# One hybrid decoder trunk, one core: recurrent output scaled in one run, query copies on their own condition, and an order planned with VectorE held while GpSimd works

## The chip, the core and the metric

The program runs on one core of one Trainium2 chip. The figure is the device time of one execution, in microseconds; for the kernel before it is 2374.19 us, the median of three runs from 2373.58 to 2376.77. In the profile the engines are PE (TensorE matmuls), PEld (its weight loads), DVE (VectorE), ACT (ScalarE), POOL (GpSimd) and SP (SyncE, here only a queue that issues transfers).

## The reference

T = 1040 tokens (16 learned ones in front of 1024) of 1024 features pass two layers, in float32.

```python
for l in range(DEPTH):
    hn = rms_norm(h, norm_mix_g[l]); proj = hn @ w_in[l]
    q, k, v, xr, gate = jnp.split(proj, splits, axis=-1)   # 512 columns each
    q = apply_partial_rope(rms_norm(q, q_norm_g[l]), cos, sin)      # 4 heads x 2 x 64; k alike
    o_attn = diff_attention(q, k, v, lam)      # softmax(q1 k1) - lam * softmax(q2 k2), causal, times v
    o_rec = rms_norm(rg_lru_branch(xr, gate, ...), rec_norm_g[l])
    h = h + jnp.concatenate([rms_norm(o_attn, ...) * (1 - lam_init), o_rec], axis=-1) @ w_out[l]
    hn = rms_norm(h, norm_ffn_g[l]); g, u = jnp.split(hn @ w_gu[l], [D_FF], axis=-1)
    h = h + (silu(g) * u) @ w_down[l]
return h[:, N_META:, :]
```

The recurrent branch is a four-tap convolution, two gates (`r`, `ig`), the scan h[t] = a[t] h[t-1] + u[t] over the tokens, a product with gelu(gate), and the norm over its 512 features with gain `rec_norm_g`.

## The kernel before, in words

**Products.** Features lie on the partitions, tokens along the free axis, in three chunks of 348, 348 and 344 columns; attention works in nine blocks of 116 tokens. Each float32 matmul is three passes over a high and a low part (`hn0h`, `hn0l` of the activations, `wh`, `wl` of the weights): high by high, low by high, high by low. One tile of a projection (`pxr`, `pgt`, `pq`, `pk`, `pv` of 128 columns and one chunk) is 24 matmuls of some 0.16 us each. High parts are made by ACT, low parts by DVE or POOL.

**Stages of a layer.** The input projections of the recurrent branch; its gates, scan and gelu; then, on the same PE queue, q, k and v of head 0; then four heads, each with its scores, softmax and value products, between which q, k, v of the next head are projected; the output projection; the FFN as seven half-size products in place of eight. In layer 0 the attention begins at about 150 us and ends at about 530, in layer 1 at about 1310 and 1740.

**Norms.** Squares are summed by tiny matmuls with a column of ones (`st_r` for the first norm, `st_q`, `st_k`, `st_y` for queries, keys and the recurrent output), the root is taken on DVE in a chain of tiny operations, and a matmul with the identity spreads it over the partitions (`bc_r`, `bck`, `bc_y`). `row` is the spread root as a tile of 128 x 1040: first that of the layer's norm, then that of the recurrent output. For a head, ACT takes the squares `csqq`, `csqk` and a scaled copy `crawq`, `crawk` out of PSUM; DVE shuffles them (`cshq`, `cshk`), POOL does the two products of the rotation with `sin` and `cos`, DVE adds them; ACT makes the high part `qh`, DVE the low part `ql`. The squares of the recurrent output are taken by ACT into one place, `sq_accy`, and summed by DVE into `accy`; so each `sq_accy` waits until DVE has added the one before.

**What sets the order.** Every piece of work is a generator, run by a `Planner` when the program is built. It keeps an assumed clock for each engine (`busy`, line 181), events, places for tiles (`get`, `free`, `lend`, `give`) and a patience for kinds of work (`turn`, with the table TURN; `idle` waits until the assumed clock of an engine stands still). Its assumed costs decide nothing but the order in which instructions are written. Each engine then executes its own instructions strictly in that order; a stalled instruction holds all behind it.

**The recurrent output** (`rec_norm`, from line 1431). hs0 to hs3 are the four blocks of 128 features. For each block in the order YN = [1, 2, 3, 0] and each chunk, DVE multiplies the block by `row` (from the second block on only when the planner's DVE clock stands still), ACT and DVE split it into a high and a low part `yo`, and POOL issues a transfer `yd<-yo` to DRAM. A block's tile then becomes a place for something else: hs2 and hs3 a second `vh` and `vl`, hs0 a second set of probability tiles `P1`, hs1 two more places for query copies (`both`). When the last chunk is out, the `row` tile becomes one more place for the tile P08, the probabilities of the last block. YO is the order in which the output projection reads the blocks.

**The query copies** (`twice`, from line 1159, in `attention`). For each block of 116 queries six transfers on the SP queue write both 64-row halves of the queries into a `view` or `both` tile that the scores `S` read. `twice` is started inside `attention`, behind a wait for the head's finished keys, queries and roots.

Of the kernel before, what the change touches and what calls it, by code (L numbers as in the profile page):

```python
# [18 lines left out]
T = 1040  # L19
# [75 lines left out]
YN = [1, 2, 3, 0]  # L95
YO = [1, 2, 0, 3]
# [37 lines left out]
class Planner:  # L134
# [5 lines left out]
    def __init__(self):  # L140
        self.heap, self.seq, self.now = [], 0, 0.0
        self.clock = {}
        self.held, self.live = {}, 0
# [37 lines left out]
    def busy(self, eng, cost, after=0.0):  # L181
        start = max(self.now, self.clock.get(eng, 0.0), after)
        self.clock[eng] = start + cost
        return start + cost

# [67 lines left out]
def nblk(i):  # L253
    return min(BQ, T - i * BQ)
# [3 lines left out]
def trunk_kernel(ctx: ExitStack, tc: tile.TileContext, h0, win, wout, wgu, wdn,  # L258
# [56 lines left out]
    def tt(out_, in0, in1, op, after=0.0, eng="V"):  # L315
        (V if eng == "V" else G).tensor_tensor(out=out_, in0=in0, in1=in1, op=op)  # L316
        n = cols(out_)
        return ready(eng, n * 1.042 + 68 if eng == "V" else n * 2.1 + 148, after)
# [8 lines left out]
    def stt(out_, in0, s, in1, op0, op1, after=0.0):  # L327
        V.scalar_tensor_tensor(out=out_, in0=in0, scalar=s, in1=in1, op0=op0, op1=op1)  # L328
        return ready("V", cols(out_) * 1.042 + 70 + 60 * aps(s), after)
# [488 lines left out]
    class Layer:  # L818
        def __init__(self, l):
# [6 lines left out]
            self.ev_q = [Event() for _ in range(HEADS)]  # L826
            self.ev_k = [Event() for _ in range(HEADS)]
# [97 lines left out]
    def qk_task(L, h, which, evs):  # L925
# [8 lines left out]
        if which == "q":  # L934
            yield from S.wait(*evs["st"])
# [3 lines left out]
            yield from S.wait(*evs["ch"])  # L939
# [151 lines left out]
    def attention(L, h):  # L1091
        yield from S.wait(L.ev_att, L.ev_q[h], L.ev_k[h], L.ev_vecs)
        l, cb, vt = L.l, L.cb, L.vt
        q, k, cq = L.q[h].parts, L.k[h].parts, L.cq[h]
        views, ev_b, nleft = {}, [Event() for _ in range(NB)], {}
# [63 lines left out]
        def twice():  # L1159

            yield from S.wait(L.ev_both[h])
            for b in range(NB):
                v = yield from S.take(L.both)
                mq = nblk(b)
                qs = slice(b * BQ, b * BQ + mq)
                for cc in range(2):
                    rows = slice(64 * cc, 64 * cc + 64)
                    for i, r in ((0, 0), (0, 64), (1, 64 * cc)):  # L1170
                        e = dma(nc.sync, v[r:r + 64, i, cc, :mq].bitcast(F32), q[i][rows, qs].bitcast(F32), 256 * mq)
                nleft[b] = 2
                views[b] = v
                S.set(ev_b[b], e)
            S.set(L.ev_both[h + 1])

# [10 lines left out]
        S.start(twice())  # L1187
# [146 lines left out]
    def rec_blocks(L):  # L1334
# [8 lines left out]
        def block(b):  # L1343
# [55 lines left out]
            e = S.busy("V", T * 2.13 + 10)  # L1399
# [36 lines left out]
    def rec_norm(L):  # L1436
# [9 lines left out]
        yield from S.wait(L.ev_att)  # L1446
        for b in YN:
            for c, (c0, cw) in enumerate(CH):
                y = L.hs[b][:, c0:c0 + cw]
                if b != YN[0]:  # L1450
                    yield from S.idle("V")
                e = tt(y, y, L.row[:, c0:c0 + cw], ALU.mult)
# [895 lines left out]
```

## Time and profile before

| | us |
|---|---|
| median of 3 runs | 2374.19 (2373.58 to 2376.77) |
| the profiled execution, its own time | 2380.8 |
| its span, first to last instruction | 2378.6 |
| PE busy | 2291.9 (96%) |
| DVE busy | 1864.1 (78%) |
| ACT / POOL busy | 1074.4 / 416.9 |
| mean granted TensorE clock | 0.979 |

The profiled execution took 6.6 us longer than the median of the timed runs, and 2.2 us of its time lie outside the span. Since PE is busy for nearly all of it, the useful readings are the stretches in which PE is not busy or in which it got a lower clock, and what PE waited for there.

### The profile page before, as it was taken

To read this page: it belongs to the slowest core of one execution; us is meant where nothing else is said; L and a number is where in the kernel's file an instruction comes from. 1 tells how busy PE (TensorE), PEld (TensorE's weight loads), DVE (VectorE), ACT (ScalarE), POOL (GpSimd) and SP (SyncE) were. 2 spreads that over 40 slices of the span, in tenths; PEclk is the share of its full clock that TensorE was granted. 3 is DMA by queue.
4 is the path that set the end of the run, shared out by engine and by line. 5 is a ranking of instruction groups with operands and counts; after the bars stand their busy time and mean duration, and the time that the engine had idled before them with its cause. 6 is when DMAs were issued, how large, how long until landed. Compare 5 with 4: busy or idle time off the path is not lost.

```text
span 2378.6 us, 40752 instructions
## 1 busy us (share of the span) xinstructions
PE 2291.9 (96%) x14514; PEld 2125.6 (89%) x14514; DVE 1864.1 (78%) x4392; ACT 1074.4 (45%) x2090; POOL 416.9 (18%) x611
## 2 busy tenths in 40 slices
PE   7998999998999999999999999999899999999998
PEld 7998898998999999999999889988688888888887
DVE  7888898888888877755976878987888888776565
ACT  4655564554333332444547555654533333335442
POOL 4134322100121200000000443230001211000000
PEclk8999999999999999999999899999999999999999
DMA  3114336323565422756521143273335654238554
GB/s 124 60 36 127 87 85 211 116 101 115 197 208 191 167 98 99 263 189 202 197 83 57 48 125 96 72 225 102 112 133 204 213 178 150 98 129 292 177 185 157
DMA packets 186539, 339.36 MB, mean 143 GB/s; under 512 B 54120, under 2 KB 75290, under 8 KB 186336
## 3 DMA queue, kind: packets, MB, share of 16 engines
q1 hardware_dynamic: 153760, 227.57, 30.1%
q0 software_dynamic: 32576, 109.19, 12.8%
q8 instruction: 114, 1.87, 0.3%
q14 instruction: 89, 0.73, 0.1%
HBM read 219.72 MB, written 95.64 MB: 133 GB/s over the span
## 4 chain that ended last, share of the span: by engine, by line
PE 80%; DVE 14%; ACT 2%; issue 2%; DMA 1%; SPq 1%; DVEq 0%; POOL 0%; ACTq 0%; POOLq 0%
PE pd L297 29%; PE pb L297 16%; PE pa L297 13%; PE po L297 3%; PE pgt L297 3%; PE pxr L297 3%; PE pv L297 3%; PE S L297 2%; PE pq L297 2%; PE pvo L297 2%; DVE P L1120 1%; PE pk L297 1%; PE atr L301 1%; PE pga L297 1%; DVE P L328 1%
## 5 line engine op out<-in xcount | busy, mean ns | idle before, releaser
L297 PE MATMUL pd<-rf,wh 128*128 128x260 f32 (+1 forms) x1848 | 414.4, 319 | 0.0
L297 PEld LDWEIGHTS pd<-rf,wh 128*128 128x128 f32 x1848 | 305.7, 188 | 27.5
L297 PE MATMUL pd<-rf,wl 128*128 128x260 f32 (+1 forms) x924 | 295.9, 320 | 0.0
L297 PEld LDWEIGHTS pd<-rf,wl 128*128 128x128 f32 x924 | 173.8, 188 | 13.8
L332 POOL DMA_DIRECT2D ad<-ct x154 | 83.0, 540 | 578.4 <-DVE ct L316 571.7
L307 ACT ACTIVATE P<-P,mx,cq 116x232 f32<-116x232 f32 (+6 forms) x144 | 124.9, 870 | 77.4 <-DVE mx L328 69.6
L316 DVE TENSOR_TENSOR ct<-pd,ct 128x260 f32<-128x260 f32 (+1 forms) x204 | 102.5, 512 | 70.8 <-PE pd L297 68.9
L297 PE MATMUL pa<-B11h,fA 128*128 128x260 f32 (+1 forms) x528 | 128.3, 324 | 19.2 <-ACT B11h L307 19.2
L316 DVE TENSOR_TENSOR ct<-pb,ct 128x260 f32<-128x260 f32 (+1 forms) x198 | 101.4, 512 | 53.9 <-PE pb L297 52.2
L316 POOL TENSOR_TENSOR wl<-wr,wh 128x512 fp32r<-128x512 f32 x70 | 97.3, 1405 | 193.2 <-ACT wh L307 163.2
L297 PE MATMUL pb<-B22h,fS 128*128 128x260 f32 (+1 forms) x528 | 126.6, 321 | 0.0
L297 PE MATMUL pb<-T1h,fS 128*128 128x260 f32 (+1 forms) x528 | 126.2, 321 | 0.0
L297 PE MATMUL pa<-B21h,fA 128*128 128x260 f32 (+1 forms) x528 | 125.7, 320 | 0.4 <-ACT ct L307 0.4
L297 PE MATMUL pb<-T2h,fS 128*128 128x260 f32 (+1 forms) x528 | 126.0, 320 | 0.0
L297 PE MATMUL pd<-T3h,fS 128*128 128x260 f32 (+1 forms) x528 | 125.9, 319 | 0.0
L297 PE MATMUL pd<-T4h,fA 128*128 128x260 f32 (+1 forms) x528 | 125.3, 319 | 0.0
L316 DVE TENSOR_TENSOR ct<-ct,ct 128x520 f32<-128x520 f32 (+2 forms) x171 | 115.9, 682 | 6.9 <-DMA ad<-ct 3.3
L297 PEld LDWEIGHTS pa<-B11h,fA 128*128 128x128 f32 x528 | 90.3, 191 | 27.5 <-ACT B11h L307 19.9
L297 PEld LDWEIGHTS pa<-B21h,fA 128*128 128x128 f32 x528 | 88.9, 188 | 8.4 <-ACT ct L307 0.9
L297 PEld LDWEIGHTS pb<-T2h,fS 128*128 128x128 f32 x528 | 89.4, 189 | 7.7
L297 PEld LDWEIGHTS pb<-T1h,fS 128*128 128x128 f32 x528 | 89.0, 188 | 7.9
L307 ACT ACTIVATE ah<-atr 116x348 fp32r<-116x348 f32 (+1 forms) x144 | 57.2, 409 | 86.0 <-PE pvo L297 46.0
(392 smaller groups left out, 7121.4 us busy)
## 6 DMA issues: line engine op xcount, KB each, us to landing
wr<-in_win_dram SPq DMA_DIRECT2D x80, 256.0 KB, 2.8
ad<-ct POOLq DMA_DIRECT2D x77, 260.0 KB, 2.7
ad<-ct POOLq DMA_DIRECT2D x77, 256.0 KB, 2.8
ct<-in_wgu_dram SPq DMA_DIRECT2D x64, 256.0 KB, 3.2
ht<-in_wgu_dram SPq DMA_DIRECT2D x60, 256.0 KB, 3.9
sq<-ad SPq DMA_DIRECT2D x58, 260.0 KB, 4.8
sq<-ad SPq DMA_DIRECT2D x58, 256.0 KB, 5.2
hw<-in_wgu_dram SPq DMA_DIRECT2D x48, 256.0 KB, 2.7
```

The costliest lines, as they stand in the source:

```text
L297: PE.matmul(out_, lhsT=lhsT, rhs=rhs, start=start, stop=stop, **(dict(skip_group_check=True) if on else {}))
L301: PE.transpose(out_, in_, idn)
L307: A.activation(out=out_, in_=in_, func=func, **kw)
L316: (V if eng == "V" else G).tensor_tensor(out=out_, in0=in0, in1=in1, op=op)
L328: V.scalar_tensor_tensor(out=out_, in0=in0, scalar=s, in1=in1, op0=op0, op1=op1)
L332: eng.dma_start(out=out_, in_=in_)
L1120: V.tensor_tensor_reduce(out=pt[:mq, k0:k0 + kw], in0=sc[:mq, :kw], in1=mask, scale=1.0, scalar=NEG if i == 0 else mx[:mq, cc, i - 1:i], o ...
```

## The change

Five things are edited.

- `YN` and `YO` become [1, 0, 2, 3]: the blocks of the recurrent output are finished, and read by the output projection, in that order.
- In `rec_norm` all twelve products with `row` come first, before the wait for the pools of the attention (`ev_att`); each takes its turn by TURN instead of waiting for a still DVE. Right behind them the tile `row` is lent to P08. The splits and transfers follow in a second loop. The first two blocks, not only the first, are staged in the places of P05 to P07.
- In the planner, POOL's tensor_tensor operations leave their assumed start and end in `S.shared`, and `behind` makes a DVE tensor_tensor or scalar_tensor_tensor whose two inputs both lie in SBUF, and the scan, start only after such an operation that is then running. This is in the plan alone: no instruction and no wait on the chip is added by it, only the order changes, for the whole program.
- `twice` is started at the head of `attention` and waits for the pools, for the previous head's copies and for a new event `ev_qt`, set when the query tiles are written. It no longer waits for the keys, the recurrent branch's vectors or the query roots.
- `row` is no longer lent at the end of `rec_norm`.

```diff
@@ -92,8 +92,8 @@
 RB = [RA, RQ, RA, RQ]
 
 YS = {2: ("vh", 1), 3: ("vl", 1), 0: ("P1", NP1), 1: None}
-YN = [1, 2, 3, 0]
-YO = [1, 2, 0, 3]
+YN = [1, 0, 2, 3]
+YO = [1, 0, 2, 3]
 NXR, NGT = 1, 5
 HR = [("r", "xr", 1), ("r", "xc", 2), ("r", "xc", 2), ("r", "r", 1), ("r", "ig", 1), ("r", "a", 1), ("r", "e2", 1),
       ("y", "hs2", 1), ("y", "hs3", 1)]
@@ -140,6 +140,7 @@
     def __init__(self):
         self.heap, self.seq, self.now = [], 0, 0.0
         self.clock = {}
+        self.shared = []
         self.held, self.live = {}, 0
 
     def start(self, gen, at=None):
@@ -183,6 +184,12 @@
         self.clock[eng] = start + cost
         return start + cost
 
+    def behind(self, after=0.0):
+
+        start = max(self.now, self.clock.get("V", 0.0), after)
+        self.shared = [x for x in self.shared if x[1] > self.now]
+        return max([start] + [b for a, b in self.shared if a <= start < b])
+
     def slots(self, pool, tag, bufs):
         if tag not in pool.slots:
             pool.slots[tag] = Slots([(0.0, pool, tag, bufs)] * bufs)
@@ -315,7 +322,13 @@
     def tt(out_, in0, in1, op, after=0.0, eng="V"):
         (V if eng == "V" else G).tensor_tensor(out=out_, in0=in0, in1=in1, op=op)
         n = cols(out_)
-        return ready(eng, n * 1.042 + 68 if eng == "V" else n * 2.1 + 148, after)
+        if eng == "V":
+            if not (in_psum(in0) or in_psum(in1)):
+                after = S.behind(after)
+            return ready(eng, n * 1.042 + 68, after)
+        e = ready(eng, n * 2.1 + 148, after)
+        S.shared.append((S.clock["G"] - n * 2.1 - 148, S.clock["G"]))
+        return e
 
     def ts(out_, in0, s1, s2, op0, op1=None, after=0.0, eng="V"):
         kw = {} if op1 is None else dict(op1=op1)
@@ -326,6 +339,8 @@
 
     def stt(out_, in0, s, in1, op0, op1, after=0.0):
         V.scalar_tensor_tensor(out=out_, in0=in0, scalar=s, in1=in1, op0=op0, op1=op1)
+        if not (in_psum(in0) or in_psum(in1)):
+            after = S.behind(after)
         return ready("V", cols(out_) * 1.042 + 70 + 60 * aps(s), after)
 
     def dma(eng, out_, in_, nbytes):
@@ -824,6 +839,7 @@
             self.q = [Block() for _ in range(HEADS)]
             self.k = [Block() for _ in range(HEADS)]
             self.ev_q = [Event() for _ in range(HEADS)]
+            self.ev_qt = [Event() for _ in range(HEADS)]
             self.ev_k = [Event() for _ in range(HEADS)]
             self.ev_v = [Event() for _ in range(HEADS)]
             self.ev_pv = [Event() for _ in range(HEADS)]
@@ -932,11 +948,12 @@
         S.start(qk_open(L, h, which, evs["tiles"]))
         S.set(evs["open"])
         if which == "q":
+            yield from S.wait(*evs["ch"])
+            S.set(L.ev_qt[h])
             yield from S.wait(*evs["st"])
             L.cq[h] = yield from S.get(small, "cq", 3, [BQ, NB, 2], F32, f"cq{l}_{h}")
             yield from rsqrt(L.cq[h], U.ss, [BQ, NB, 2], f"q{l}_{h}")
             S.free(S.now, U.ss)
-            yield from S.wait(*evs["ch"])
             S.set(L.ev_q[h])
             return
         for c in range(3):
@@ -1089,10 +1106,31 @@
 
 
     def attention(L, h):
+        views, ev_b, nleft = {}, [Event() for _ in range(NB)], {}
+
+        def twice():
+
+
+
+            yield from S.wait(L.ev_att, L.ev_qt[h], L.ev_both[h])
+            q = L.q[h].parts
+            for b in range(NB):
+                v = yield from S.take(L.both)
+                mq = nblk(b)
+                qs = slice(b * BQ, b * BQ + mq)
+                for cc in range(2):
+                    rows = slice(64 * cc, 64 * cc + 64)
+                    for i, r in ((0, 0), (0, 64), (1, 64 * cc)):
+                        e = dma(nc.sync, v[r:r + 64, i, cc, :mq].bitcast(F32), q[i][rows, qs].bitcast(F32), 256 * mq)
+                nleft[b] = 2
+                views[b] = v
+                S.set(ev_b[b], e)
+            S.set(L.ev_both[h + 1])
+
+        S.start(twice())
         yield from S.wait(L.ev_att, L.ev_q[h], L.ev_k[h], L.ev_vecs)
         l, cb, vt = L.l, L.cb, L.vt
         q, k, cq = L.q[h].parts, L.k[h].parts, L.cq[h]
-        views, ev_b, nleft = {}, [Event() for _ in range(NB)], {}
         lsum = yield from S.get(small, "lsum", 2, [BQ, NB, 2], F32, f"lsum{l}_{h}")
         G.memset(lsum, 1.0)
         a_ev = [Event() for _ in range(NB)]
@@ -1156,24 +1194,6 @@
 
         left = [NB]
 
...
         def all_scores():
             yield from S.wait(L.ev_p1[h])
             for qb in range(NB):
@@ -1184,7 +1204,6 @@
                 S.start(block(qb, tiles[qb], P1, None))
             S.set(L.ev_p1[h + 1])
 
-        S.start(twice())
         S.start(all_scores())
         yield from S.wait(L.ev_v[h])
         v = L.v[h]
@@ -1396,7 +1415,7 @@
             hs = yield from S.get(L.cy, f"hs{b}", 1, [P, WY[b]], F32, f"hs{l}_{b}")
             hs = hs[:, :T]
             V.tensor_tensor_scan(out=hs, data0=a, data1=ig, initial=0.0, op0=ALU.mult, op1=ALU.add)
-            e = S.busy("V", T * 2.13 + 10)
+            e = S.busy("V", T * 2.13 + 10, S.behind())
             S.free(e, a, ig)
             L.hs[b] = hs
             S.set(L.ev_hs[b], e + LAT)
@@ -1443,15 +1462,23 @@
         S.set(L.ev_rec2)
         yield from S.wait(*there)
         S.free(S.now, ry)
-        yield from S.wait(L.ev_att)
+
+        scaled = {}
         for b in YN:
             for c, (c0, cw) in enumerate(CH):
                 y = L.hs[b][:, c0:c0 + cw]
-                if b != YN[0]:
-                    yield from S.idle("V")
-                e = tt(y, y, L.row[:, c0:c0 + cw], ALU.mult)
-                yield e + LAT
-                tag = f"P0{5 + c}" if b == YN[0] else "oh"
+                yield from S.turn("V", "r")
+                scaled[b, c] = tt(y, y, L.row[:, c0:c0 + cw], ALU.mult) + LAT
+        yield from S.wait(L.ev_att)
+        S.lend(S.clock["V"], const, "row", S.slots(L.cb, f"P0{NB - 1}", 0))
+        for b in YN:
+            for c, (c0, cw) in enumerate(CH):
+                y = L.hs[b][:, c0:c0 + cw]
+                if b not in YN[:2]:
+                    yield from S.turn("V", "r")
+                if scaled[b, c] > S.now:
+                    yield scaled[b, c]
+                tag = f"P0{5 + c}" if b in YN[:2] else "oh"
                 st = yield from S.get(L.cb, tag, 1, [P, 2, CW], F32R, f"yo{l}_{b}{c}")
                 e = yield from split(st[:, 0, :cw], st[:, 1, :cw], y, L.vt[:, V_REC + b:V_REC + b + 1], kind="r")
                 yield e + LAT
@@ -1464,7 +1491,6 @@
                 for i in range(2):
                     place_view(L, both[:, i])
             S.set(L.ev_y[b], e)
-        S.lend(e, const, "row", S.slots(L.cb, f"P0{NB - 1}", 0))
 
 
     def open_layer(L):
```

No instruction is added or removed as work (PE has 11738 rows in both programs), but the order moves everywhere. Three places show how. A row is line, operation, written tile, read tiles, shape.

**The start, DVE.** `hn0l` is the low part of the normed input; its number names the eighth of the features (109, 111, ... 123) and the tile it reads names the chunk (`hr_133`, `hr_135` chunk 0, `hr_144`, `hr_146`, `hr_148` chunk 1, `hr_150`, `hr_153`, `hr_156` chunk 2). In the program before, the low parts of chunk 1 stand together:

```order
L328 SCALAR_TENSOR_TENSOR hn0l_109<-hr_144,vec_87,hn0h_108 128x348
L328 SCALAR_TENSOR_TENSOR hn0l_111<-hr_144,vec_87,hn0h_110 128x348
L328 SCALAR_TENSOR_TENSOR hn0l_113<-hr_144,vec_87,hn0h_112 128x348
L328 SCALAR_TENSOR_TENSOR hn0l_115<-hr_146,vec_87,hn0h_114 128x348
L328 SCALAR_TENSOR_TENSOR hn0l_117<-hr_146,vec_87,hn0h_116 128x348
L328 SCALAR_TENSOR_TENSOR hn0l_121<-hr_148,vec_87,hn0h_120 128x348
L328 SCALAR_TENSOR_TENSOR hn0l_119<-hr_146,vec_87,hn0h_118 128x348
L328 SCALAR_TENSOR_TENSOR hn0l_123<-hr_148,vec_87,hn0h_122 128x348
```

In the changed program the eighth numbered 119 of chunk 1 (`hn0l_119<-hr_146`) stands 18 rows further back, behind a stretch that holds chunk 2's parts, the root of chunk 0 (`ms_r`, `re`, `rr`, `nq_r`) and the low part `gwl` of a gate weight. The last of it reads:

```order
L335 TENSOR_SCALAR rr_106<-ms_r_302 116x3
L341 SCALAR_TENSOR_TENSOR hn0l_123<-hr_148,vec_87,hn0h_122 128x348
L323 TENSOR_TENSOR nq_r_315<-rr_106 116x3
L341 SCALAR_TENSOR_TENSOR hn0l_121<-hr_156,vec_87,hn0h_120 128x344
L323 TENSOR_TENSOR nq_r_315<-nq_r_315,ms_r_302 116x3
L341 SCALAR_TENSOR_TENSOR hn0l_111<-hr_150,vec_87,hn0h_110 128x344
L341 SCALAR_TENSOR_TENSOR nq_r_315<-nq_r_315 116x3
L323 TENSOR_TENSOR gwl_190<-wr_0_307,gwh_189 128x512
L341 SCALAR_TENSOR_TENSOR rr_106<-nq_r_315,rr_106 116x3
L323 TENSOR_TENSOR gwl_190<-wr_1_311,gwh_189 128x512
L341 SCALAR_TENSOR_TENSOR nq_r_315<-rr_106 116x3
L341 SCALAR_TENSOR_TENSOR hn0l_119<-hr_146,vec_87,hn0h_118 128x348
```

PE's matmuls of `pxr_01` (chunk 1) with `hn0h_118` and `hn0l_119`, which stood at its rows 64 to 66, stand at 73 to 75, behind the nine sums `st_r` of chunk 0.

**The opening of layer 0's attention, ACT.** Before, the squares `csqk` of the first two chunks of keys stand behind squares of the recurrent output (`sq_accy`) and high parts of the queries (`qh`), which wait for DVE:

```order
L307 ACTIVATE sq_accy_1517<-hs_2_1428 128x348
L307 ACTIVATE qh_0_1360<-crawq_01_1446 128x348
L307 ACTIVATE sq_accy_1545<-hs_2_1428 128x344
L307 ACTIVATE sq_accy_1561<-hs_3_1391 128x348
L307 ACTIVATE csqk_00_1563<-pk_00_1486 128x348
L307 ACTIVATE crawk_00_1564<-pk_00_1486,vec_87 128x348
L307 ACTIVATE qh_0_1360<-crawq_00_1404 128x348
L307 ACTIVATE sq_accy_1581<-hs_3_1391 128x348
L307 ACTIVATE qh_0_1360<-crawq_02_1501 128x344
L307 ACTIVATE sq_accy_1615<-hs_3_1391 128x344
L307 ACTIVATE csqk_01_1627<-pk_01_1553 128x348
L307 ACTIVATE crawk_01_1628<-pk_01_1553,vec_87 128x348
```

After:

```order
L314 ACTIVATE csqq_02_1498<-pq_02_1437 128x344
L314 ACTIVATE crawq_02_1500<-pq_02_1437,vec_87 128x344
L314 ACTIVATE sq_accy_1505<-hs_2_1423 128x348
L314 ACTIVATE csqk_00_1545<-pk_00_1485 128x348
L314 ACTIVATE crawk_00_1546<-pk_00_1485,vec_87 128x348
L314 ACTIVATE qh_0_1360<-crawq_00_1404 128x348
L314 ACTIVATE sq_accy_1565<-hs_2_1423 128x348
L314 ACTIVATE qh_0_1360<-crawq_01_1448 128x348
L314 ACTIVATE csqk_01_1602<-pk_01_1535 128x348
L314 ACTIVATE crawk_01_1603<-pk_01_1535,vec_87 128x348
L314 ACTIVATE sq_accy_1606<-hs_2_1423 128x344
```

The squares of key chunk 0 now stand behind one `sq_accy` and no `qh`, those of chunk 1 behind one more `sq_accy` and two `qh`; the rest of `sq_accy` is behind them. PE's order follows: `st_y`, the sums over `accy`, moves from its rows 809 to 817 to rows 885 to 892, behind the value projection. In layer 1 ACT's order changes in the same way.

**The scores of head 0 in layer 1, PE.** `S_0010` and `S_0000` are the scores of block 0. Before, they stand in the second query tile of head 1 (`pq_11`):

```order
L297 MATMUL pq_11_16557<-hnh_2_13146,wl_16285 128x348
L297 MATMUL pq_11_16557<-hnh_3_13148,wh_16284 128x348
L297 MATMUL pq_11_16557<-hnl_3_13149,wh_16284 128x348
L297 MATMUL pq_11_16557<-hnh_3_13148,wl_16285 128x348
L297 MATMUL S_0010_16583<-kl_0_16037,view_16256 116x116 x2
L297 MATMUL S_0000_16586<-kh_0_16036,view_16256 116x116 x2
L297 MATMUL pq_11_16557<-hnh_4_13937,wh_16284 128x348
L297 MATMUL pq_11_16557<-hnl_4_13938,wh_16284 128x348
```

After, they stand 62 rows later, between the first and the second key tile of head 1:

```order
L304 MATMUL pk_10_16607<-hnh_7_14433,wh_16415 128x348
L304 MATMUL pk_10_16607<-hnl_7_14434,wh_16415 128x348
L304 MATMUL pk_10_16607<-hnh_7_14433,wl_16416 128x348
L304 MATMUL S_0010_16684<-kl_0_16031,view_16386 116x116 x2
L304 MATMUL S_0000_16687<-kh_0_16030,view_16386 116x116 x2
L304 MATMUL pk_11_16692<-hnh_0_13142,wh_16415 128x348
L304 MATMUL pk_11_16692<-hnl_0_13143,wh_16415 128x348
L304 MATMUL pk_11_16692<-hnh_0_13142,wl_16416 128x348
```

In layer 0 they stand at row 950 in both. The scores of block 8 of head 0, whose probabilities use the place lent from `row`, move from PE's row 1335 to 1191 in layer 0, and from 8326 to 8217 in layer 1.

More of the change, by code (lines that the diff above doesn't have):

```diff
@@ L1157, in attention @@
         left = [NB]
[L1159 to L1175, printed above, removed]
         def all_scores():
```

## The prediction

> **What bounds the kernel now.** First the page's head, busy times and the chain that ended last:
>
> ```profile
> span 2378.6 us, 40752 instructions
> PE 2291.9 (96%) x14514; PEld 2125.6 (89%) x14514; DVE 1864.1 (78%) x4392; ACT 1074.4 (45%) x2090; POOL 416.9 (18%) x611
> PE 80%; DVE 14%; ACT 2%; issue 2%; DMA 1%; SPq 1%; DVEq 0%; POOL 0%; ACTq 0%; POOLq 0%
> ```
>
> PE is idle for 2378.6 - 2291.9 = 86.7 us, and all work on it stays. So a gain can only come from that idle time, or from time at a low clock. Next the windows (start and end, length, busy us of PE, PEld, DVE, ACT, POOL, then granted clock, DMA share, GB/s):
>
> ```profile
> 0.00:60.00 60.00, 47.19 (x228) 44.19 (x229) 44.87 (x98) 25.07 (x46) 26.81 (x30) 0.86 0.38 124
> 60.00:150.00 90.00, 89.68 (x569) 89.01 (x568) 70.13 (x96) 63.17 (x93) 17.23 (x16) 1.00 0.16 51
> 150.00:190.00 40.00, 34.04 (x207) 32.54 (x205) 36.47 (x109) 17.58 (x41) 21.95 (x29) 0.87 0.25 71
> 190.00:560.00 370.00, 343.69 (x2331) 335.53 (x2330) 315.83 (x1061) 203.97 (x456) 90.27 (x120) 0.96 0.39 119
> 560.00:1300.00 740.00, 740.00 (x6008) 739.92 (x6006) 565.70 (x1119) 300.11 (x546) 73.86 (x141) 1.00 0.48 162
> 1320.00:1360.00 40.00, 35.18 (x193) 34.50 (x191) 35.01 (x97) 14.61 (x33) 19.82 (x22) 0.79 0.13 36
> 1360.00:1680.00 320.00, 301.50 (x1932) 280.87 (x1932) 260.81 (x949) 173.60 (x411) 89.87 (x120) 0.98 0.40 119
> ```
>
> From 60 to 150 and from 560 to 1300 PE works without a gap: these stretches pass a shift on, unchanged. The losses lie in four places: the start; layer 0's opening of attention (150 to 190: 40 - 34.04 = 5.96 us idle, and 13% of 34 busy us, 4.4, to the clock); layer 1's (1320 to 1360: 4.82 idle, 21% of 35.2, 7.4, clock); and the heads between. The change's order moves work in all four.
>
> **The start.** The timeline of 17 to 57 us (start, length, engine, line, operation; in brackets the idle time ahead and what ended it):
>
> ```profile
> 17.31 16.53 DVE L328 SCALAR_TENSOR_TENSOR hn0l<-hr,vec,hn0h 128x348 fp32r<-128x348 f32 x14
> 25.04 10.74 POOL L316 TENSOR_TENSOR hr<-hr 128x1044 f32<-128x1044 f32 x8 [0.95 <-DVE hn0l L328]
> 37.12 0.56 DVE L328 SCALAR_TENSOR_TENSOR hn0l<-hr,vec,hn0h 128x344 fp32r<-128x344 f32 x1
> 36.51 0.68 DVE L316 TENSOR_TENSOR wl<-wr,wh 128x512 fp32r<-128x512 f32 x1
> 33.75 0.32 PE L297 MATMUL pxr<-hn0h,wl 128*128 128x344 f32 x1
> 39.37 3.25 PE L297 MATMUL st_r<-sums,hr 128*116 128x2 f32 x16 [2.34 <-ACT hr L307]
> 54.04 0.64 PE L297 MATMUL pxr<-hn0h,wh 128*128 128x344 f32 x1
> 56.59 0.40 PE L297 MATMUL pgt<-hn0h,wh 128*128 128x348 f32 x1
> 40.00:50.00 10.00, 10.00 (x47) 9.94 (x48) 4.48 (x23) 1.49 (x3) 0.00 (x0) 0.50 0.20 68
> ```
>
> Beside POOL a low part takes 16.53 / 14 = 1.18 us, without POOL 0.56. PE pauses from 34.07 to 39.37, apart from two sums, then runs at clock 0.50 until 54, and begins `pgt` at 56.59. In the changed order `hn0l_119` of chunk 1 is DVE row 37. Ahead of it, from row 10 (about 13.5 us), stand 15 low parts (17.7 us at 1.18), four weight low parts (0.7 to 1.4 each: 2.8 to 5.6) and some ten tiny operations (0.15 to 0.2 each alone: 2): it runs at 36 to 38.5, I take 37. PE comes to the matmul that needs it at about 27, since 45 fewer matmuls of 0.16 stand ahead of it than were done by 34. So it pauses ten us, earlier, with more work behind: 81 matmuls at 0.16 (13.0), two groups of sums (3.8) and three spreads (1.2), 18.0 in all. At full clock `pgt` begins at 55.0. A clock of 0.50 adds 0.13 per matmul while it lasts. If as long as before, 15 us, it adds 7, and `pgt` begins at 62. But there the sums cut the low stretch twice, and here the first 33 matmuls hold only one spread among them; I take half of that, 3.5: 58.5. **+2 us**, bounds -1.5 and +6; 60 to 150 passes it on.
>
> On this the Trainium skill ("TensorE: Matmul & The Clock Gate", "What's actually happening") says that about 3.4 us of sustained work bring the full rate back. By that rule the pause would cost 1.6 in place of 3.5, and this term were 0; the trace's 15 us do not agree with it, if the sums count as work.
>
> **The openings of attention.** PE's waits from 150 to 200 (us in total, times, longest), then from 1310 to 1370, then rows of the timeline, and the window of 1350 to 1360:
>
> ```profile
> PE st_q L297 <- ACT csqq L307: 2.1, 1, 2.1
> ...
> PE st_k L297 <- ACT csqk L307: 1.4, 1, 1.4
> ...
> PE st_q L297 <- POOL csqq L997: 2.6, 1, 2.6
> PE st_k L297 <- ACT csqk L307: 2.2, 1, 2.2
> ...
> 166.42 0.49 ACT L307 ACTIVATE sq_accy<-hs 128x344 f32<-128x344 f32 x1 [2.00 <-DVE accy L316]
> 149.37 4.38 DVE L316 TENSOR_TENSOR hs<-hs,gt 128x348 f32<-128x348 f32 x4
> 153.68 0.50 DVE L316 TENSOR_TENSOR gt<-pgt,row 128x344 f32<-128x344 f32 x1
> 170.63 0.55 DVE L328 SCALAR_TENSOR_TENSOR cb<-nq_k,ck 116x384 f32<-116x384 f32 x1
> 187.87 0.51 DVE L316 TENSOR_TENSOR hs<-hs,row 128x348 f32<-128x348 f32 x1
> 189.03 0.58 DVE L328 SCALAR_TENSOR_TENSOR yo<-hs,vec,yo 128x348 fp32r<-128x348 f32 x1 [0.23 <-ACT yo L307]
> 190.94 0.32 PE L297 MATMUL pq<-hn0h,wh 128*128 128x348 f32 x1
> 1350.00:1360.00 10.00, 10.00 (x46) 9.69 (x45) 6.36 (x36) 2.78 (x6) 3.07 (x4) 0.56 0.09 26
> ```
>
> The squares of the keys come late because ACT stands in front of an `sq_accy` that waits for DVE. I walked the changed order with these durations. The last gate tile (`gt`) goes ahead of the products it stood behind, 153.7 to about 151, so `csqq` is ready at 153, 1.6 earlier; the key squares no longer hold PE for more than half a us; `st_y`, `bc_y` and their chain stand behind the value projection. PE reaches the first `bck` at about 166.5, and waits there for DVE's `cb`, which has 22 rows to go from 160: 170.5, 4 us, the largest wait left. From there 70 matmuls at 0.16 bring it to `pq` at 182: 8.9 earlier than 190.9, of which I leave 0.9 for the clock behind the 4 us wait. **-8**, bounds -10 (the 5.96 idle and the 4.4 of clock) and -3 (the first two `st` waits alone). The nine products with `row` that came later than the first three, 9 x 0.51 = 4.6 us of DVE, now stand ahead of the scores, and the splits `yo`, 0.58 each, behind: hidden under the PE work of head 1's projection, and 4.6 us if they were not. YN and YO by themselves cost nothing: the twelve splits and transfers are the same, and the output projection reads them over 200 us later.
>
> In layer 1 the 2.6 us for `csqq` stay: the clearing on POOL still stands behind rotations. The 2.2 for `csqk` go, and some of the 7.4 of clock, of which the 4.4 from 1350 to 1360 (10 us at 0.56) stand behind that wait. I take 2.8 of the 4.4. **-5**, bounds -8 and -1.
>
> **The heads.** The stretch with the most DVE in it, PE's waits in layer 0, and the first transfers of query copies with the weight load behind them:
>
> ```profile
> 200.00:380.00 180.00, 164.04 (x1099) 158.33 (x1098) 162.20 (x603) 102.98 (x251) 63.87 (x77) 0.96 0.35 98
> PE S L297 <- DVE mx L1120: 4.0, 4, 1.8
> PE bco L623 <- DVE nq_k L316: 3.4, 1, 3.4
> PE st_k L297 <- DVE crawk L316: 3.3, 1, 3.3
> 190.78 1.66 SPq L332 DMA_DIRECT2D view<-qh  x2
> 202.77 2.04 SPq L332 DMA_DIRECT2D wr<-in_win_dram  x2
> ```
>
> Here DVE is 90% and PE 91% busy: neither is alone the bound. The changed order lets block 8 of head 0 begin 144 rows earlier and moves other blocks either way. PE's idle time from 190 to 560 is 26.3 us, from 1360 to 1680 18.5; the three longest waits of layer 0 are 10.7 of it. I found no rows that say which of them go, and put **0**, bounds -13 (half of 26.3) and +13 (all that the openings give, given back). The copies of a block take 3.7 us of SP and hold the weight load behind them, 12 us in the row above; in the changed order they wait for less, and the first of them go ahead of the second and third chunk of the keys. I put 0 for it, with 3.7 us on the other side.
>
> **The sum.** +2 - 8 - 5 + 0 = -11. The profiled execution at 2380.8 would become 2369.8; it stood 6.6 above the median 2374.2, so the forecast for the median is **2363 us**.
>
> **The rivals.**
>
> *The heads gain as well.* For it: beside POOL an operation with both inputs in SBUF doubles (1.18 against 0.56), POOL works 63.87 of the 180 us, and the new plan knows it. Against: the chip is as slow, and only a better filling could help. With half of layer 0's 26.3 us (13) the time is 2350.
>
> *The scores come too late in layer 1: slower.* `S` of block 0 moves back 62 matmuls, 62 x 0.16 = 9.9 us of PE time, more than the 5 gained ahead. DVE has little to do meanwhile and owes the softmax of head 0 to the later heads. If DVE bounds there, layer 1 ends 5 us later than now (+5 in place of -5); with layer 0's gain lost in the same manner to 90% busy DVE (0 in place of -8) the sum is +2 + 5 = +7: 2381. It decides from the point where DVE is busy for over 90% from 1360 to 1680; it is at 260.81 / 320 = 82% now, which speaks against it.
>
> The Trainium skill ("SBUF — State Buffer", "Who interferes with whom") has it that a VectorE operation with two SBUF inputs and a GpSimd operation that reads SBUF block each other for a whole instruction, whichever starts first. The 1.18 us beside POOL agree with that; by this rule the sum of both engines' work is the same in any order, and the plan's hold by itself gains nothing unless other work fills the gap.
>
> *The hold changes the order, not the waits: about the same.* Half of the opening's gain (-4 and -2) is all that is left, since DVE is 36.47 of 40 us busy there and `cb` waits for it anyway, and the start costs 5: -1, 2373.
>
> **How the numbers follow.** A measurement of this kernel can tell 0.2%, 4.7 us. Forecast: 0.45, in a range of its own of 2357 to 2369. Heads too: 0.16. Scores too late: 0.2. About the same: 0.19. The range 2350 to 2381 takes in the start's bounds, the heads' gain and the slower rival up to its price. Faster: 0.45 + 0.16 less a little for a forecast that falls short, 0.6; slower 0.21; same 0.19.
>
> **What would show it.** Start: PE pauses from about 27 to 37 and `pgt` begins at 58.5 (55 to 62). Layer 0: no wait of `st_k` for `csqk` over a us; a wait of `bck` for `cb` of some 4 us near 167; `pq` of head 1 at 182 plus the start's shift. Layer 1: the wait for `csqk` gone, that for POOL's `csqq` still there. Heads: PE idle 190 to 560 within some 12 us of 26. Wrong if PE's idle time in the heads has grown by more than both openings gave, or if `pgt` begins after 63.

## The result

The changed kernel takes 2358.27 us, the median of four runs (2354.46 to 2362.03), against 2375.48 for the kernel before (four runs, 2373.58 to 2379.03): 17.2 us less. The ratio of the runs is 0.9918 with a 95% interval of 0.9905 to 0.9931 (the two medians alone give 0.9928). The forecast was 2363 and faster. The profiled execution took 2362.0 us, its span is 19.3 us shorter than that of before. The head of its page, its busy times and its chain:

```profile
span 2359.3 us, 40740 instructions
PE 2275.6 (96%) x14514; PEld 2110.9 (89%) x14514; DVE 1858.9 (79%) x4392; ACT 1072.9 (45%) x2090; POOL 423.1 (18%) x611
PE 83%; DVE 11%; issue 2%; ACT 2%; DMA 1%; POOL 0%; SPq 0%; DVEq 0%; ACTq 0%; POOLq 0%
```

The number of matmuls is the same. PE is idle for 2359.3 - 2275.6 = 83.7 us, 3.0 less than before, and the work that it does took 16.3 us less: most of the gain is clock, not idle time. Laid over PE's busy time, the granted clock of the two traces costs PE 39.4 us before and 27.3 in the changed kernel: 4.8 and then 1.7 in layer 0's opening, 8.5 and then nothing in layer 1's, 9.7 and 4.9 in layer 0's heads, but 7.7 and 13.0 in layer 1's. The windows, columns as in the prediction:

```profile
0.00:60.00 60.00, 42.99 (x240) 40.69 (x241) 47.50 (x97) 25.64 (x46) 26.89 (x30) 0.83 0.39 126
150.00:190.00 40.00, 36.88 (x245) 35.94 (x245) 34.91 (x110) 17.11 (x43) 19.26 (x23) 0.96 0.26 72
190.00:560.00 370.00, 347.10 (x2403) 338.27 (x2403) 321.11 (x1082) 208.60 (x463) 93.17 (x125) 0.97 0.39 122
1320.00:1360.00 40.00, 38.62 (x265) 37.73 (x265) 36.23 (x114) 19.76 (x47) 20.41 (x24) 1.00 0.28 76
1360.00:1680.00 320.00, 299.36 (x1844) 275.36 (x1843) 263.51 (x941) 174.92 (x405) 87.45 (x115) 0.96 0.40 122
```

Windows at fixed times cut different work in two kernels. So the stages are measured from the timeline of PE, by the first matmul of a kind: `pk` of head 0 (the opening begins), `pq` of head 1 (the heads begin), and the first `pb` of the FFN. In us, with the difference to before:

| profiled execution | to `pk` of head 0 | opening, layer 0 | heads, layer 0 | opening, layer 1 (from `pq`) | heads, layer 1 | span |
|---|---|---|---|---|---|---|
| before | 150.0 | 40.9 | 355.3 | 56.2 | 353.7 | 2378.6 |
| changed | -2.3 | -6.5 | -6.9 | -11.8 | +8.0 | -19.3 |

"Heads" here reaches from the second head's projection over the output projection to the first FFN products; what lies between and behind differs by under 1.6 us in every run below. Each such row is read from one execution. Where two of the kernels below have the same order of matmuls in a stage, the stage's times agree to 2.6 us or better: the five that share the order of both openings with the changed kernel have -6.4 to -8.0 and -11.7 to -12.2 there. But the execution of the kernel before stands some 5 us above its median, and no other run has its order in the openings or the heads.

The changed kernel's pause at the start and the two rows that bound its opening of layer 0, and PE's waits from 150 to 200 and from 1290 to 1360:

```profile
35.16 0.66 PE L304 MATMUL pxr<-hn0l,wh 128*128 128x348 f32 x1 [5.59 <-DVE hn0l L341]
147.68 0.32 PE L304 MATMUL pk<-hn0h,wh 128*128 128x348 f32 x1
182.14 0.42 PE L304 MATMUL pq<-hn0h,wh 128*128 128x348 f32 x1 [1.00 <-ACT vraw L314]
```

```profile
PE st_q L304 <- POOL csqq L1014: 1.6, 1, 1.6
PE pq L304 <- ACT vraw L314: 1.0, 1, 1.0
PE st_y L304 <- DVE crawk L323: 0.5, 1, 0.5
...
PE bc_y L638 <- DVE nq_y L323: 0.7, 1, 0.7
PE st_q L304 <- POOL csqq L1014: 0.5, 1, 0.5
```

No wait for the key squares `csqk` of more than 0.3 us is left in either opening, and in layer 1 the clock is 1.00 where it was 0.79.

### The profile page after: what moved, and what is told of

The parts are those of the page before. It is cut to its first block, busy times and chain, and to the rows that moved or that the text cites. A ratio compares the mean times of both kernels' runs of the same rounds, so it can differ in the third digit from the quotient of the medians.

```text
span 2359.3 us, 40740 instructions
## 1 busy us (share of the span) xinstructions
PE 2275.6 (96%) x14514; PEld 2110.9 (89%) x14514; DVE 1858.9 (79%) x4392; ACT 1072.9 (45%) x2090; POOL 423.1 (18%) x611
## 4 chain that ended last, share of the span: by engine, by line
PE 83%; DVE 11%; issue 2%; ACT 2%; DMA 1%; POOL 0%; SPq 0%; DVEq 0%; ACTq 0%; POOLq 0%
PE pd L304 29%; PE pb L304 16%; PE pa L304 13%; PE pxr L304 4%; PE po L304 3%; PE pgt L304 3%; PE pq L304 3%; PE pvo L304 2%; PE S L304 2%; DVE P L1158 2%; PE pk L304 2%; PE pv L304 1%; PE atr L308 1%; PE pga L304 1%; DVE P L341 1%
## 5 line engine op out<-in xcount | busy, mean ns | idle before, releaser
L314 ACT ACTIVATE P<-P,mx,cq 116x116 f32<-116x116 f32 (+5 forms) x144 | 124.6, 867 | 79.3 <-DVE mx L341 67.6
L304 PEld LDWEIGHTS pd<-T3h,fS 128*128 128x128 f32 x528 | 89.0, 188 | 8.0
```

What stands on the lines that cost most here:

```text
L304: PE.matmul(out_, lhsT=lhsT, rhs=rhs, start=start, stop=stop, **(dict(skip_group_check=True) if on else {}))
L314: A.activation(out=out_, in_=in_, func=func, **kw)
```

## The experiments

All twelve are set against runs of the kernel before on the same chip. First the parts apart. "Hold" is the planner's rule for VectorE beside GpSimd.

**The hold alone.** The edit: of the change's diff only the planner's part.

```diff
+        if eng == "V":
+            if not (in_psum(in0) or in_psum(in1)):
+                after = S.behind(after)
...
+            e = S.busy("V", T * 2.13 + 10, S.behind())
```

> The kernel before with the planner's hold alone (VectorE operations with both inputs in SBUF planned behind a running GpSimd operation); the recurrent output, the block order and the query copies are as before. In its order the squares of the keys stand ahead of most squares of the recurrent output in layer 0, and `hn0l_119` stands at VectorE's row 37, as in the changed kernel. Theory 1 (the hold's order pays in the start and the two openings, nothing else does): start 1.8 us earlier, first query matmul of head 1 some 8 us earlier in layer 0 and some 20 in layer 1, total 2360 (15 us less than before). Theory 2 (the openings are given back in the heads unless the recurrent output and the copies are moved as well): the same openings, but PE's idle time in the heads grows by as much; total 2370 or more.

Measured: 2389.86 against 2376.86, ratio 1.0055 (1.0042 to 1.0067): 13 us slower. Theory 1 is wrong, theory 2 has the way right, and more so than it said. Both openings are shorter by as much as in the changed kernel (-7.3 and -12.1), but the heads give back 6.9 and 24.6 us. Windows of this run, and PE's waits from 190 to 300:

```profile
220.00:230.00 10.00, 6.68 (x44) 5.50 (x43) 10.00 (x28) 6.36 (x15) 3.88 (x4) 0.99 0.46 132
230.00:240.00 10.00, 9.25 (x45) 9.22 (x46) 6.51 (x29) 3.58 (x8) 0.91 (x3) 0.67 0.53 156
250.00:260.00 10.00, 5.35 (x41) 4.76 (x39) 8.37 (x21) 6.05 (x17) 3.29 (x4) 1.00 0.32 106
```

```profile
PE S L304 <- DVE mx L1135: 8.9, 4, 5.6
PE atr L308 <- DVE mx L341: 3.4, 1, 3.4
PE atr L308 <- DVE P L341: 2.4, 1, 2.4
```

PE has head 1's projection behind it 17 us earlier than before (`pq` of head 2 at 232.4 against 249.6), and then waits for the softmax of head 0 on DVE, which has not come forward with it.

**Everything but the hold.** The edit: GpSimd operations are not entered in the planner's list.

```diff
-        S.shared.append((S.clock["G"] - n * 2.1 - 148, S.clock["G"]))
```

> The changed kernel with the planner's hold taken out: GpSimd operations are not entered in the list, so nothing is planned behind them. All twelve products first, the early row tile, the block order and the early query copies stay. The order of the start and of both openings falls back to that of before. Theory 1: 2373 (within 4 us of before), pgt at 56.6, pq of head 1 at 191. Theory 2: 2367, since the heads lose less idle time by the three other edits.

Measured: 2375.93 against 2376.86, ratio 0.9994 (0.9984 to 1.0003): no difference. The opening of layer 0 is -0.2, that of layer 1 -3.8. So the hold's order is needed for all of the first and for two thirds of the second, and the other edits together are worth nothing without it.

**The recurrent output in one run alone, and the early copies alone.** The edits: the change's hunks in `rec_norm`; its hunks on `ev_qt` and `twice`.

```diff
+        scaled = {}
+        for b in YN:
...
+        S.lend(S.clock["V"], const, "row", S.slots(L.cb, f"P0{NB - 1}", 0))
```

> The kernel before with the edit of the recurrent output alone: twelve products with `row` first, the tile lent right behind them, two blocks staged in the places of P05 to P07; block order, copies and plan as before. The start and openings are as before to the row. Theory 1: 2375, within 3 us. Theory 2: 4 to 8 us less, all of it in the heads, where block 8 of head 0 stands 71 rows earlier in layer 0 and 48 in layer 1.

> The kernel before with the query copies alone moved: they wait for the query tiles, not for keys, roots and vectors. The scores of block 0 stand 32 rows earlier in both layers. Theory 1: 2375, within 3 us. Theory 2: 3 to 6 us less, in the heads; if the copies hold weight loads on the SP queue, 4 us more.

Measured: 2383.58, ratio 1.0025 (1.0013 to 1.0037), and 2382.05, ratio 1.0023 (1.0014 to 1.0032): both slower, by some 6 us, against both theories. The loss stands in layer 1's heads (+7.5 and +9.3).

**The hold with one of the two.** The edits are the hold's hunks with those of the copies, or with those of `rec_norm`, both under the old block order.

```diff
+        yield from S.wait(L.ev_att, L.ev_qt[h], L.ev_both[h])
```

> The kernel before with the hold and the early query copies; recurrent output and block order as before. With the hold alone PE ran out of ready work from 220 to 280 us, since head 1's projection was done before the scores of head 0 had begun: the scores of block 0 stood 37 rows later than before; here 6. Theory A (the hold needs scores early, which the copies give): most of the loss of the hold alone goes, total 2362. Theory B (the hold needs VectorE free of the recurrent output's splits, which the scaling in one run gives): still slower than before, 2385.

> The kernel before with the hold and the products of the recurrent output in one run; copies and block order as before. The scores of block 0 stand 87 rows later than before in both layers. Theory A: slower than the hold alone or like it, 2390 or more, PE idle from 200 to 300 by over 15 us. Theory B: 2362.

Measured: 2388.36, ratio 1.0045 (1.0029 to 1.0060), and 2388.02, ratio 1.0038 (1.0021 to 1.0055). Neither takes the loss of the hold away, so both theories as put are wrong: neither early scores nor the scaling are enough. In the second PE is idle for 10.5 us from 200 to 300, not for over 15 as theory A had it.

**The reason for the openings, by itself.** One wait in the plan of the kernel before, without the hold:

```diff
+            if b >= 2:
+                yield from S.wait(L.ev_ksq)
             yield from L.accy.add(b, c, y)
...
+            if which == "k" and h == 0 and c == 1:
+                S.set(L.ev_ksq, e)
```

> The kernel before, without the hold, with one added condition in the plan: the squares of the last two blocks of the recurrent output are taken only after the squares of the second chunk of head 0's keys. It tests the reason given for the openings by itself. If the late key squares were what held PE there, head 1's first query matmul comes 4 to 6 us earlier in layer 0 and 5 to 10 in layer 1, and the wait of `st_k` for `csqk` is gone, with the start as before; total 2367 if the heads pass it on, 2376 if they give it back. If the openings gained by the hold in another way, the shift there is under 2 us.

Measured: 2388.03 against 2375.87, ratio 1.0042 (1.0028 to 1.0056). The openings are shorter by 2.4 and 5.3 us, less than half of 6.5 and 11.8. PE's waits there (146 to 186, then 1312 to 1360) show why:

```profile
PE st_k L297 <- ACT csqk L307: 2.3, 1, 2.3
PE st_q L297 <- ACT csqq L307: 2.1, 1, 2.1
PE bck L623 <- DVE cb L328: 1.8, 2, 1.4
...
PE bck L623 <- DVE cb L328: 3.7, 1, 3.7
PE st_q L297 <- POOL csqq L998: 2.6, 1, 2.6
```

One wait for `csqk` is still there, and `bck` now waits for DVE. The late key squares are a part of the cause in layer 0; in layer 1 that is less clear, since the runs above without the hold have -1.0 to -3.8 as well. The hold moves more: the gate tile's product earlier, `bck` behind the value projection's beginning. Which of these gives the rest was not tried apart. The heads of this run give back 17.0 us in layer 1, so the total says nothing for the openings.

**The hold in the openings only.** The changed kernel, with the hold off in the plan from head 0's attention of a layer to the next layer's opening.

```diff
+        return start if self.off else max([start] + [b for a, b in self.shared if a <= start < b])
...
+        S.off = True
         l, cb, vt = L.l, L.cb, L.vt
```

> The changed kernel with the hold in the plan only until head 0's attention of a layer begins, and again from the next layer's opening on; the heads, the output projection and the FFN are planned without it. Start and openings as in the changed kernel to the row. If the hold pays in the openings alone: 2358, within 3 us of the changed kernel. If it costs in the heads, as the hold alone did: 2352. If it pays in the heads too: 2364.

Measured: 2356.91 against 2375.87, ratio 0.9913 (0.9896 to 0.9931), as the changed kernel. That was the number for a hold that pays in the openings alone, but it comes from two differences: the heads are +0.6 and -4.3 here, against -6.9 and +8.0: the hold helps in layer 0's heads and hurts in layer 1's.

**What keeps the heads from giving the openings back.** Three single edits of the changed kernel taken back: the row tile lent late, the old block order, the late copies.

```diff
-        S.lend(S.clock["V"], const, "row", S.slots(L.cb, f"P0{NB - 1}", 0))
...
             S.set(L.ev_y[b], e)
+        S.lend(e, const, "row", S.slots(L.cb, f"P0{NB - 1}", 0))
```

> The changed kernel with one line moved back: the tile `row` is lent to the probabilities of block 8 only after the last split and transfer, as before. Block 8 of head 0 then stands at PE's row 1315 in place of 1191, everything up to block 6 of head 0 as in the changed kernel. Theory P (what feeds VectorE early in the heads is the place for block 8): most of the gain goes, 2375 to 2385. Theory Q (it is the second place for the probabilities P1, which the new block order gives early): 2358 to 2364.

```diff
-YN = [1, 0, 2, 3]
-YO = [1, 0, 2, 3]
+YN = [1, 2, 3, 0]
+YO = [1, 2, 0, 3]
```

> The changed kernel with the old block order, YN = [1, 2, 3, 0] and YO = [1, 2, 0, 3]; all else stays. The tile of the recurrent block hs0, which becomes the second place for the probabilities P1, is then free last and not second. Blocks 4, 6 and 8 of head 0 stand at rows 1132, 1217 and 1358 in place of 1072, 1134 and 1191. Theory Q: the gain goes, 2380 to 2390, with VectorE busy for under 95 of the 110 us from 190 to 300 (101 in the changed kernel, 90 before). Theory P: within 5 us of the changed kernel, 2358 to 2363.

```diff
-            yield from S.wait(L.ev_att, L.ev_qt[h], L.ev_both[h])
+            yield from S.wait(L.ev_both[h])
```

> The changed kernel with the query copies as before, behind keys and roots; hold, scaling, early row tile and new block order stay. The scores of block 0 stand 87 rows later than in the changed kernel in layer 0 and 25 later in layer 1, block 8 of head 0 28 rows later. Theory Q with late scores: part of the gain goes, 2366 to 2374. If early copies are needed for it at all: 2385 or more, as with hold and scaling under the old block order.

(In the last, `twice` also stands behind `attention`'s wait again, as before.) Measured: row late 2406.11, ratio 1.0128 (1.0114 to 1.0142); old block order 2370.45, ratio 0.9980 (0.9970 to 0.9990); late copies 2376.66, ratio 1.0004 (0.9995 to 1.0013), all against 2375.70. Against the changed kernel that is some 48, 12 and 18 us. Each of the three is needed, and late copies lie between the two outcomes that were named for them; theory P had the row right in sign, but far too small, theory Q had the block order right in sign, and too large, and the sign that it named did not come: DVE is busy for 97.6 of the 110 us, not for under 95. The run with the old block order is also the hold, the scaling and the copies together: 5 us faster than before, where the hold with either one was 12 us slower.

With late copies, PE's waits from 190 to 560 us have a copy of queries in second place, in layer 0's last head at 430.8 us; in the changed kernel the longest wait for a copy there is 2.0 us:

```profile
PE S L304 <- DMA view<-qh: 6.3, 1, 6.3
```

That is a third of the 17.8 us by which layer 0's heads are longer in that run than in the changed kernel; the rest is spread over smaller waits and a lower clock.

The row tile is the largest. DVE's and ACT's waits in that run from 190 to 300 us, and DVE's in the changed kernel:

```profile
DVE yo L341 <- ACT yo L314: 11.2, 2, 6.0
...
ACT yo L314 <- DMA yd<-yo: 6.1, 1, 6.1
...
ACT yo L314 <- DMA od<-oh: 3.7, 1, 3.7
```

```profile
DVE yo L341 <- ACT yo L314: 1.0, 2, 0.8
```

The last splits stand in the middle of the heads in both kernels: the last four of layer 0 begin on DVE at 247.0, 252.5, 258.4 and 269.6 in the changed kernel, and at 240.0, 253.5, 263.7 and 270.4 here. What the late tile takes away is the softmax work between them: 7, 14 and 45 other DVE instructions in the changed kernel, 19, 5 and none here. The last two stand next to each other on DVE:

```profile
263.69 0.70 DVE L341 SCALAR_TENSOR_TENSOR yo<-hs,vec,yo 128x348 fp32r<-128x348 f32 x1 [5.21 <-ACT yo L314]
270.36 0.58 DVE L341 SCALAR_TENSOR_TENSOR yo<-hs,vec,yo 128x344 fp32r<-128x344 f32 x1 [5.97 <-ACT yo L314]
```

The late splits pass through one staging place, which the attention's output `oh` uses too. So a high part waits on ACT for the transfer ahead of it (the 6.1 and 3.7 us above), DVE stands behind it with all its softmax work, and PE's projection behind ACT's reading of PSUM: PE waits 8.4 us in layer 0 and 13.1 in layer 1 for `crawq`.

The windows of 190 to 300 us show how far DVE has work; before, the changed kernel, the hold alone, the row late, in this order, one fence each:

```profile
190.00:300.00 110.00, 99.77 (x651) 96.10 (x650) 89.76 (x321) 61.45 (x146) 44.55 (x53) 0.95 0.36 102
```

```profile
190.00:300.00 110.00, 102.53 (x696) 98.73 (x695) 101.11 (x387) 69.85 (x166) 45.47 (x57) 0.95 0.37 106
```

```profile
190.00:300.00 110.00, 91.69 (x579) 87.85 (x578) 93.59 (x310) 56.53 (x134) 42.92 (x53) 0.91 0.34 100
```

```profile
190.00:300.00 110.00, 95.39 (x574) 91.87 (x573) 78.02 (x288) 55.24 (x134) 42.20 (x53) 0.84 0.33 97
```

The changed kernel's DVE does 101.1 us of work here and executes 387 instructions, against 89.8 and 321; with the row late it is 78.0. What it does not do here it owes at the end of the heads: the last value product of layer 0's attention ends 20.5 us earlier in the changed kernel, 2.8 with the hold alone, and 5.5 later with the row late. It is no law: with late copies DVE is busy for 98.0 of these 110 us, and the heads still give back 10.9; with the hold in the openings only it is busy for 103.7, the most of all, and layer 0's heads gain nothing (+0.6); and without the hold the last value product ends 18.1 us earlier, with no gain either (+0.5). Whether the place for P1 is what makes the block order count was not tried apart.

**A version that beats both.** The orders of the two runs above put together: the hold everywhere but in layer 1's attention and behind it.

```diff
-        S.off = True
+        S.off = L.l == 1
```

> The changed kernel with the hold in the plan everywhere but in layer 1's attention and behind it. Its order is that of the changed kernel up to the scores of layer 1, and from there that of the run with the hold in the openings alone. Layer 0's heads took 7 us less than before in the changed kernel, against 0.6 more with the hold in the openings alone; layer 1's heads 8 more against 4.3 less. If these are properties of the orders and add up: 2346 to 2351, better than both. If they were the chance of one profiled execution each: 2357.

Measured: 2348.06 against 2375.70, ratio 0.9888 (0.9872 to 0.9903): 27.6 us less than before and some 10 less than the changed kernel. The stages add up: -6.4, -6.6, -11.7 and -5.7, a span 33.0 us shorter. So the stage times of the two runs were properties of their orders and not the chance of one execution each. Its windows of layer 1's heads:

```profile
1360.00:1500.00 140.00, 129.37 (x894) 123.91 (x893) 130.23 (x497) 87.80 (x215) 51.68 (x65) 0.99 0.38 107
1500.00:1640.00 140.00, 135.82 (x840) 121.63 (x840) 111.93 (x414) 71.29 (x167) 32.20 (x45) 1.00 0.47 147
```

DVE works for 130.2 of the first 140 us, 120.9 in the changed kernel, and the clock stays at 0.99 and 1.00, where the changed kernel has 0.94 and 0.96.

All runs by stage, in us against before (one execution each), with the ratio of all their runs:

| run | ratio | opening 0 | heads 0 | opening 1 | heads 1 |
|---|---|---|---|---|---|
| changed | 0.9918 | -6.5 | -6.9 | -11.8 | +8.0 |
| hold alone | 1.0055 | -7.3 | +6.9 | -12.1 | +24.6 |
| all but the hold | 0.9994 | -0.2 | +0.5 | -3.8 | +2.4 |
| one run of scaling alone | 1.0025 | -0.8 | +2.2 | -3.4 | +7.5 |
| copies alone | 1.0023 | 0.0 | -4.0 | -1.0 | +9.3 |
| hold and copies | 1.0045 | -6.4 | +7.5 | -12.2 | +20.2 |
| hold and scaling | 1.0038 | -7.4 | +7.3 | -9.5 | +21.8 |
| squares later, no hold | 1.0042 | -2.4 | -3.2 | -5.3 | +17.0 |
| hold in the openings only | 0.9913 | -6.4 | +0.6 | -11.8 | -4.3 |
| row late | 1.0128 | -8.0 | +17.7 | -11.8 | +31.4 |
| old block order | 0.9980 | -6.5 | -1.0 | -11.8 | +10.3 |
| late copies | 1.0004 | -7.5 | +10.9 | -12.1 | +7.1 |
| hold not in the last heads | 0.9888 | -6.4 | -6.6 | -11.7 | -5.7 |

## Why the prediction was right, and where it was not

The sum was -11 and the medians moved by -17.2, the spans by -19.3. The way was right, and the two openings carry the gain, as forecast. That the number lies in its range of 2357 to 2369, by 1.3 us, is in part luck: the start came out 4 us and layer 1's opening 7 us better than their terms, and the heads' 0 is the sum of two errors.

- **The start, +2: wrong in sign against this execution of before, and small.** PE does wait for `hn0l_119`, but for 5.6 us and not ten: it ends at 35.2, with DVE's row 37 two us earlier than walked and PE's 72 rows done later, at 29.6. The clock was back at 1.00 from 40, so `pgt` begins at 54.8, 1.8 earlier. The last section shows that the 56.6 of before was the worse of two cases; against the better one, 52.4, the changed kernel is 2.4 later. So the runs do not settle the sign.
- **Layer 0's opening, -8: right, -6.5.** The path was another than walked: no wait of `bck` for `cb` was there at all (4 us were walked), and `st_q` waited 1.6 for POOL's clearing.
- **Layer 1's opening, -5: the term that was mis-sized most, -11.8**, outside its bounds of -8 to -1. The wait for `csqk` went as said. The wait for POOL's `csqq`, which was said to stay, fell from 2.6 to 0.5. And all of the clock's loss went, not 2.8 of it: 0.79 to 1.00 over 1320 to 1360. The prediction had weighed 2.8 of the 4.4 us behind one wait, where the whole stretch had 7.4 to give. Some of the -11.8 may be that one execution of before: without the hold there are -1.0 to -3.8.
- **The heads, 0: right in sum (+1.1), by two errors of opposite sign** (-6.9 and +8.0), and for no reason that the prediction gave: luck. Most of both is clock (4.8 us less and 5.3 more lost to it, as said above). The prediction's bound of -13 also took half of 26.3 us of idle time in which 9.0 us are one wait of `pa`, the FFN's first product, for ACT's `B11h`. That is longer than each of the three waits that it named, and it is 9.0 in the changed kernel too.
- **The edits costed at nothing are the ones without which the result is lost.** "YN and YO by themselves cost nothing": taking them back costs 12 us. Early copies, put at 0: 18 us. The early row tile, named only by the rows that it moves: 48 us. The products and splits are the same, as the prediction said; what it missed is that places and the order of the heads depend on them. By themselves, without the hold, these edits do cost nothing (2375.93).
- **The slower rival** had the right question (the gain of the openings is given back by the softmax) in the wrong kernel: it is what the hold does alone, with 31.5 us given back in both layers. Its sign, DVE over 90% busy from 1360 to 1680, was not the one to watch: it was 82% in both kernels and 81% with the hold alone, where the loss did come. DVE idle early in the heads goes with the largest loss (78.0 of 110 us with the row late), but is no sure sign either, as the hold in the openings only shows.
- **The rule of the Trainium skill in "SBUF — State Buffer", "Who interferes with whom"**, by which the hold gains nothing by itself in shared work, agrees with the runs: with the hold alone DVE is busy for 1874.0 us and POOL for 424.8, against 1864.1 and 416.9 before; in the changed kernel it is 1858.9 and 423.1. The hold pays by which work it puts first.

## What to carry to other kernels

In this kernel a planner's rule that shortened one stage brought work forward on the engine that bounds that stage, and not on the one that bounds the next; look at once at the engine that bounds the next stage, and at the places and transfers that let it start earlier. Edits to such an order need not add up one by one (here scaling, copies and hold are +7, +5 and +13 us apart and -5 together, -17 with the block order, which was not run by itself), so test the whole with single parts taken back, not only the parts alone, and split the time by stages before judging a total. Where two orders differ by stage, try the better stages of both together: here each kept its time (-6.6 after -6.9, and -5.7 after -4.3).

## What the runs showed of the hardware

After the pause in the start, the time at the clock of 0.50 is not fixed by the order. In the kernel before and in the run with the squares later, PE has the same matmuls in the same order up to `pgt`. The windows of 45 to 50 us, before and then the squares later:

```profile
45.00:50.00 5.00, 5.00 (x26) 4.94 (x25) 0.52 (x1) 0.46 (x1) 0.00 (x0) 0.50 0.00 0
```

```profile
45.00:50.00 5.00, 5.00 (x39) 4.96 (x38) 2.23 (x14) 0.96 (x4) 0.00 (x0) 0.92 0.00 0
```

The clock is 0.50 in one and 0.92 in the other, and `pgt` begins at 56.6 and 52.4. Of the five profiled runs that have this part of the order from before on PE, three begin `pgt` at 56.5 to 56.9 and two at 52.4; the nine with the hold's order lie between 53.5 and 55.2. The Trainium skill ("TensorE: Matmul & The Clock Gate", "What's actually happening") gives some 3.4 us of sustained work for the return to the full clock, and a free-running window: the runs agree with a chance in it, but the low clock lasted up to 16 us here, while sums of 2 columns stood between the matmuls. The sums stand there in all five, so by themselves they do not decide it; whether they play a part was not tried.
